# Holding ScalarE's splits of late weights behind squares and results, and moving one Strassen product to the ring of four PSUM banks

## The chip, the core and the metric

The kernel runs on one core of a Trainium2 chip. The metric is the device time of one execution in microseconds (us). Before the change the median of three runs is 2169.33 us (2167.87 to 2173.09).

## What is computed

A decoder trunk of two layers on 512 prompt tokens and 8 × 8 sample tokens (T = 576 columns), model width 1024. The reference, cut to the part around the change:

```python
def decoder_layer(x, pos, states, lw):
    y, new_states = token_mixing(_rmsnorm(x, lw['attn_norm']), pos, states, lw)
    x = x + y.astype(x.dtype)                 # y = merged @ w_out
    h = _rmsnorm(x, lw['ffn_norm'])
    g, u = jnp.split(h @ lw['w_ffn_in'], 2, axis=-1)
    x = x + ((jax.nn.silu(g) * u) @ lw['w_ffn_out']).astype(x.dtype)
    return x, new_states
```

`w_ffn_in` is 1024 × 5632, `w_ffn_out` 2816 × 1024. Token mixing has four recurrent mixers; the change does not touch them.

## The kernel before, in words

Activations lie transposed: 128 channels on the partitions, tokens along the row, in two halves of HW = 288 columns. Every product is made of float16 parts: a weight or activation is split into a high half (ScalarE, L227, L247, L1695) and a low half (VectorE, L228, L249, L1696), and TensorE adds three products, high·high, high·low and low·high (L240 to L242, L1726 to L1728). A full 128 × 128 block of weights therefore costs three matmuls of 288 columns per half.

**Weights.** `wload` (L207) brings a matrix of `nk` blocks in groups of 512 columns of 128 rows: a DMA on SP's queue into one of four `raw` tiles (L219), ScalarE's split (L227) and VectorE's low half (L228), which frees the raw tile. The split tiles come from rings of SBUF ("w" 4, "gs" 6, "r2" 4, "gd" 4, "u" 23, "rd" 2).

**Around the change, per layer, in the order of the program:**

- `out_proj` (L1562): eight row blocks m of `w_out`, two halves each. `part(m, w, half)` makes 24 matmuls into a bank of ring "b" (tile `ob`); `add_x` (L1550) then adds the residual on VectorE (L1553), squares on ScalarE (`sq`, L430), and VectorE adds the squares up (L435). Blocks 0 to 3 go half by half, then blocks 4 to 7 first half, then blocks 4 to 7 second half. The first three FFN matrices (`ffn_weights`, gate and up columns, four groups each) are loaded ahead of the last eight parts.
- `norm_half` (L453): one matmul with ones over the sum of squares (`rps`, L446), a table load pinned to its place in ScalarE's queue (L439), Ln and Exp, a second table load, then eight tiles of `h` (VectorE L469, ScalarE L470, low half on VectorE or GpSimd L471). For the first half it is traced behind part (4, second half).
- `ffn` (L1759): FFN blocks 0 to 2 with plain matmuls (`up`, tile `fb`), 48 per half; after the first the norm of the second half and GpSimd's differences of the activations (`strassen_tokens`). Blocks 3 to 21 are "units" of a Strassen scheme (`strassen`, L1716) with seven products of 12 matmuls, A11, A12, A22, S2, S1, S3, S4, each into one PSUM bank, and seven sums on VectorE (`plus`, L1742, tiles `su` and `sc`). A11 is copied out by ScalarE (L1747), S1's bank is read by u4 and c22, A22's by c21. The unit's weights come from `strassen_weights` two units ahead (load) and in the course of the unit before and the unit itself (seven splits, L1695 and L1696; two accumulating DMAs and two sums on GpSimd). `gated` (L1765) makes silu(g)·u on ScalarE (L1771) and VectorE (L1773) and splits it (L247, L249).
- The down stage: `weights(m)` is a `wload` of one row block of `w_ffn_out` (22 blocks in six groups), `down(m, w, half)` 66 matmuls per half (tile `xb`).

PSUM has eight banks: ring "b" of four, "g" of two, "r" of two. In the FFN's Strassen units A11, A12 and S2 take "b", A22 and S1 "g", S3 and S4 "r". `last_gates` calls the same function for the mixers' gates.

**What sets the order.** The program is traced as above, but the framework's scheduler writes each engine's queue: it runs the trace through a model of the times and takes the instruction that comes first in the program among those that the model has ready. An instruction whose inputs the model sees early moves up in its engine's queue. On the chip every queue is executed in order. `keep_in_program_order` adds an edge of order (not a wait) to the instruction traced before on the same engine; `add_manual_dep` with `NoSync` adds such an edge to a chosen instruction.

Of the kernel before, what the change touches and what calls it, by code (L numbers as in the profile page):

```python
# [25 lines left out]
KT = D // 128  # L26
WS = 256.0
# [121 lines left out]
def result(steps):  # L149

    while True:
        try:
            next(steps)
        except StopIteration as e:
            return e.value
# [18 lines left out]
class Net:  # L174
# [29 lines left out]
        return self.pc[:, c:c + 1]  # L204


    def wload(self, pieces, nk, ncols, rings=("w",)):  # L207


        nc = self.nc  # L210
        step = GW // ncols
        tiles, parts = [], []
        for g, k0 in enumerate(range(0, nk, step)):
            kn = min(step, nk - k0)
            n = kn * ncols
            raw = self.wp.tile([128, GW], F32, tag="raw", name="raw")
            rv = raw[:, :n].rearrange("p (k c) -> p k c", k=kn)
            for ap, off, w in pieces:
                nc.sync.dma_start(out=rv[:, :, off:off + w],  # L219
                                  in_=ap[128 * k0:128 * (k0 + kn)].rearrange("(k p) c -> p k c", p=128))  # L220
            if not parts:
                ring, rings = rings[0], rings[1:] or rings
                c = SIZE[ring] // (4 * GW)
                hl = self.t(ring, [128, c, 2, GW], "whl", F16)
                parts = [hl[:, i] for i in range(c)]
            hl = parts.pop(0)
            nc.scalar.activation(hl[:, 0, :n], raw[:, :n], AF.Copy, scale=WS)  # L227
            nc.vector.scalar_tensor_tensor(hl[:, 1, :n], raw[:, :n], WS, hl[:, 0, :n], op0=MUL, op1=SUB)  # L228
            tiles.append(hl[:, :, :n].rearrange("p a (k c) -> p a k c", k=kn))
        return lambda k: (tiles[k // step][:, 0, k % step], tiles[k // step][:, 1, k % step])  # L230
# [13 lines left out]
    def split(self, out_hi, out_lo, src, scale=1.0):  # L244

        nc = self.nc
        nc.scalar.activation(out_hi, src, AF.Copy, scale=scale)  # L247
        if scale == 1.0:
            nc.vector.tensor_tensor(out_lo, src, out_hi, op=SUB)  # L249
        else:  # L250
            nc.vector.scalar_tensor_tensor(out_lo, src, scale, out_hi, op0=MUL, op1=SUB)
# [1233 lines left out]
    def last_gates(self, l):  # L1485
# [34 lines left out]
        for i, (q, bi, name, m) in enumerate(pairs):  # L1520
            if i + 1 < len(pairs):
                next(prep[i + 1])

            def steps():
                for s in range(7):
                    if s < 4:
                        next(prep[i])
                    if s > 2 and i + 1 < len(pairs):
                        next(prep[i + 1])
                    yield  # L1530
            c = yield from self.strassen(self.sw[i], lambda j, k: [self.T4[2 * j + k // 2][:, k % 2, p] for p in range(2)],
                                         steps(), "b" if q == 2 else "r", "e", lambda a: nc.scalar.activation(a, a, AF.Tanh, scale=0.5 * PH))
            nwb = branch(pairs[i + 1][1], pairs[i + 1][3]) if i + 1 < len(pairs) else None
            for j, half in ((0, 0), (1, 1), (1, 0), (0, 1)):
                hs = slice(half * HW, half * HW + HW)
                th, mg = c[2 * j + half], self.mg[m + j]
                if q == 3 and half == j:
                    self.mh[m + j] = self.t("rs" if m < 6 else "u", [128, 2, T], f"mh{m + j}", F16)
                ps = self.psum("b", [128, HW], "ub")
                run(self.gemm(ps, lambda k: wb[k], range(2), 128 * j, 128, self.hl_rhs(self.bo[name], half)))  # L1540
                u = self.t("e", [128, HW], "gu")
                nc.vector.scalar_tensor_tensor(u, th, 1.0, ps, op0=ADD, op1=MUL)  # L1542
                nc.gpsimd.tensor_tensor(mg[:, hs], mg[:, hs], u, op=ADD)
                if q == 3:
                    mh = self.mh[m + j]
                    self.split(mh[:, 0, hs], mh[:, 1, hs], mg[:, hs], 0.5 * PA * AS)
                yield
            wb = nwb
# [13 lines left out]
    def out_proj(self, l):  # L1562

        nc, t = self.nc, self.io

        def weights(m, rings):
            return self.wload([(t["w_out"][l][:, 128 * m:128 * m + 128], 0, 128)], KT, 128, rings)

        def part(m, w, half):
            ps = self.psum("b", [128, HW], "ob")  # L1570
            run(self.gemm(ps, w, range(KT), 0, 128, self.hl_rhs(self.mh, half)))
            self.add_x(m, half, ps, True)
        for m in range(4):
            self.load_x(m)
            w = weights(m, ("w",))
            for half in range(2):
                part(m, w, half)
        ws = {}
        for m in range(4, KT):
            self.load_x(m)  # L1580
            ws[m] = weights(m, ("gd",))
        self.wf = [self.ffn_weights(l, m, r) for m, r in enumerate(("w", "gs", "r2"))]
        for half in range(2):
            for m in range(4, KT):
                part(m, ws[m], half)
                if half == 1 and m == 4:
                    self.norm_half("ffn_norm_w", l, 0, True)

    def ffn_weights(self, l, m, ring):
        return [self.wload([(self.io["w_ffn_in"][l][:, o + 128 * m:o + 128 * m + 128], 0, 128)], KT, 128, (ring,))  # L1590
                for o in (0, DFF)]

    def mix_units(self, l, then=None):
# [119 lines left out]
            split(name, a)  # L1713
            yield

    def strassen(self, w, t, prep, ps3, ring, then=None):  # L1716


        nc = self.nc
# [17 lines left out]
        def tt(i):  # L1737
            return lambda k: t(i, k)
# [9 lines left out]
        c11 = plus(p1, (yield from product("b", "A12", b(4, h0))), "sc11")  # L1748
        p4 = yield from product("g", "A22", tt(3))
        u2 = plus(p1, (yield from product("b", "S2", tt(1))), "su2", SUB)  # L1750
        p5 = yield from product("g", "S1", tt(0))
        u4 = plus(u2, p5, "su4")
        u3 = plus(u2, (yield from product(ps3, "S3", tt(2))), "su3")
        c22 = plus(u3, p5, "sc22")
# [4 lines left out]
    def ffn(self, l):  # L1759
# [56 lines left out]
        for m in range(3, nm):  # L1816
            if len(prep) > 2:
                next(prep[2])
            now, then = prep[0], prep[1] if len(prep) > 1 else None
            prep.pop(0)  # L1820

            def steps():
                for q in range(7):
                    if q < 4:
                        next(now)
                    if q > 2 and then:
                        next(then)
                    yield
            w = self.sw[m]
            g0, g1, u0, u1 = result(self.strassen(w, lambda i, k: (T4[i][:, k, 0], T4[i][:, k, 1]), steps(), "r", "gt"))  # L1830
            gated(m, 0, g0, u0)
            gated(m, 1, g1, u1)

        def weights(m, rings=("w",)):
            return self.wload([(t["w_ffn_out"][l][:, 128 * m:128 * m + 128], 0, 128)], nm, 128, rings)

        def down(m, w, half, then=None):
            ps = self.psum("b", [128, HW], "xb")
# [112 lines left out]
```

## Time and profile before

| | |
|---|---|
| median of three runs | 2169.33 us |
| the profiled execution, its own time | 2174.78 us |
| its span in the profile | 2173.0 us |
| `out_proj`, layers 0 and 1: first and last matmul of `ob` | 647.0 to 702.1, ending 1769.8 in layer 1 |
| Strassen units of the FFN, to the first matmul of `xb` in layer 0 | 745.4 to 960.2 |

The page of the profile gives busy times per engine; PE is TensorE, DVE VectorE, ACT ScalarE, POOL GpSimd, SP the engine that issues most DMAs. "Idle before" is the time in which an engine waited ahead of an instruction, and the name behind the arrow is what ended that wait. PEclk is the granted share of TensorE's 2.4 GHz, which switches between 1.2 and 2.4.

### The profile page before, as it was taken

To read this page: it belongs to the slowest core of one execution; us is meant where nothing else is said; L and a number is where in the kernel's file an instruction comes from. 1 tells how busy PE (TensorE), PEld (TensorE's weight loads), DVE (VectorE), ACT (ScalarE), POOL (GpSimd) and SP (SyncE) were. 2 spreads that over 40 slices of the span, in tenths; PEclk is the share of its full clock that TensorE was granted. 3 is DMA by queue.
4 is the path that set the end of the run, shared out by engine and by line. 5 is a ranking of instruction groups with operands and counts; after the bars stand their busy time and mean duration, and the time that the engine had idled before them with its cause. 6 is when DMAs were issued, how large, how long until landed. Compare 5 with 4: busy or idle time off the path is not lost.

```text
span 2173.0 us, 42394 instructions
## 1 busy us (share of the span) xinstructions
PE 2028.8 (93%) x15754; PEld 1603.7 (74%) x15754; DVE 1587.5 (73%) x3385; ACT 1089.7 (50%) x2534; POOL 630.3 (29%) x889
## 2 busy tenths in 40 slices
PE   7999999998998999999999899989898989989998
PEld 5777887786777677777777678768776767767776
DVE  7888757668786899863488986675778678998441
ACT  6564546355555555442466455463755455554332
POOL 2213222136541534310012132213464224332000
PEclk9999999999999999999999999999999999999999
DMA  6312214324545455453421222242354544554431
GB/s 183 80 47 63 69 50 112 87 75 107 133 121 174 102 139 134 106 142 111 117 74 51 60 72 57 74 118 62 85 137 116 151 128 112 141 136 108 124 110 49
DMA packets 381274, 223.68 MB, mean 103 GB/s; under 512 B 60674, under 2 KB 361274, under 8 KB 381068
## 3 DMA queue, kind: packets, MB, share of 16 engines
q1 hardware_dynamic: 365516, 192.66, 31.6%
q0 software_dynamic: 15552, 28.32, 7.6%
q8 instruction: 124, 2.03, 0.4%
q14 instruction: 82, 0.67, 0.1%
HBM read 173.65 MB, written 16.59 MB: 88 GB/s over the span
## 4 chain that ended last, share of the span: by engine, by line
PE 50%; DVE 22%; ACT 9%; issue 8%; DMA 6%; POOL 2%; SPq 1%; DVEq 0%; ACTq 0%; POOLq 0%
PE pb L242 5%; PE pb L241 5%; PE pb L240 5%; PE xb L241 4%; PE xb L242 4%; PE xb L240 4%; PE fsS L1728 2%; PE fsS L1726 2%; PE fsS L1727 2%; DVE fy L1773 2%; DVE hA L1696 2%; DVE hS L1696 2%; DVE sc L1742 2%; DVE su L1742 2%; PE lvp L1018 2%
## 5 line engine op out<-in xcount | busy, mean ns | idle before, releaser
L240 PE MATMUL pb<-h,whl 128*128 128x288 f16 (+1 forms) x1504 | 433.7, 289 | 4.0 <-ACT whl L227 2.1
L242 PE MATMUL pb<-h,whl 128*128 128x288 f16 (+1 forms) x1504 | 434.0, 289 | 3.2 <-DVE whl L228 3.1
L241 PE MATMUL pb<-h,whl 128*128 128x288 f16 (+1 forms) x1504 | 433.9, 289 | 0.4 <-DVE h L471 0.2
L228 DVE SCALAR_TENSOR_TENSOR whl<-raw,whl 128x512 f16<-128x512 f32 (+1 forms) x352 | 243.1, 699 | 138.9 <-ACT whl L227 137.0
L242 PEld LDWEIGHTS <-whl 128*128 128x128 f16 (+1 forms) x2784 | 274.2, 98 | 85.4 <-issue 9.2
L241 PEld LDWEIGHTS <-whl 128*128 128x128 f16 (+1 forms) x2784 | 273.7, 98 | 82.0 <-issue 6.0
L240 PEld LDWEIGHTS <-whl 128*128 128x128 f16 (+1 forms) x2784 | 276.2, 99 | 76.4 <-issue 3.6
L227 ACT ACTIVATE whl<-raw 128x512 f16<-128x512 f32 (+1 forms) x352 | 212.7, 617 | 171.7 <-PE pb L242 50.4
L241 PE MATMUL xb<-fa,whl 128*128 128x288 f16 x704 | 201.6, 286 | 0.0
L240 PE MATMUL xb<-fa,whl 128*128 128x288 f16 x704 | 201.6, 286 | 0.0
L242 PE MATMUL xb<-fa,whl 128*128 128x288 f16 x704 | 201.6, 286 | 0.0
L1726 PE MATMUL fsS<-st,hS 128*128 128x288 f16 x456 | 132.5, 291 | 6.9 <-ACT hS L1695 6.9
L1726 PE MATMUL fsA<-h,hA 128*128 128x288 f16 x432 | 123.7, 286 | 12.2 <-DVE gu L1542 10.0
L1728 PE MATMUL fsS<-st,hS 128*128 128x288 f16 x456 | 132.4, 290 | 0.4 <-DVE hS L1696 0.3
L1727 PE MATMUL fsS<-st,hS 128*128 128x288 f16 x456 | 132.5, 291 | 0.0
L1728 PE MATMUL fsA<-h,hA 128*128 128x288 f16 x432 | 123.7, 286 | 0.8 <-DVE hA L1696 0.8
L1727 PE MATMUL fsA<-h,hA 128*128 128x288 f16 x432 | 123.7, 286 | 0.0
L1695 ACT ACTIVATE hS<-sraw 128x512 f16<-128x512 f32 x130 | 79.8, 623 | 63.3 <-POOL sraw L1710 42.5
L1726 PEld LDWEIGHTS <-hS 128*128 128x128 f16 x864 | 85.5, 99 | 34.9 <-ACT hS L1695 12.9
L1696 DVE SCALAR_TENSOR_TENSOR hS<-sraw,hS 128x512 f16<-128x512 f32 x130 | 103.5, 800 | 9.2 <-ACT hS L1695 8.3
L1696 DVE SCALAR_TENSOR_TENSOR hA<-sraw,hA 128x512 f16<-128x512 f32 x110 | 96.6, 888 | 13.1 <-ACT hA L1695 13.1
L1728 PEld LDWEIGHTS <-hS 128*128 128x128 f16 x864 | 85.3, 99 | 24.8 <-DVE hS L1696 2.4
(481 smaller groups left out, 5172.8 us busy)
## 6 DMA issues: line engine op xcount, KB each, us to landing
raw<-in_w_in SPq DMA_DIRECT2D x208, 256.0 KB
sraw<-in_w_ffn_in SPq DMA_DIRECT2D x40, 512.0 KB
raw<-in_w_ffn_out SPq DMA_DIRECT2D x80, 256.0 KB
raw<-in_w_ffn_in SPq DMA_DIRECT2D x78, 256.0 KB
sraw<-sraw POOLq DMA_DIRECT2D x40, 256.0 KB, 3.6
x<-xd SPq DMA_DIRECT2D x32, 288.0 KB
raw<-sraw POOLq DMA_DIRECT2D x34, 256.0 KB, 3.3
sraw<-in_w_in SPq DMA_DIRECT2D x32, 256.0 KB
```

The costliest lines, as they stand in the source:

```text
L227: nc.scalar.activation(hl[:, 0, :n], raw[:, :n], AF.Copy, scale=WS)
L228: nc.vector.scalar_tensor_tensor(hl[:, 1, :n], raw[:, :n], WS, hl[:, 0, :n], op0=MUL, op1=SUB)
L240: nc.tensor.matmul(ps, wh, hi, start=i == 0, stop=False)
L241: nc.tensor.matmul(ps, wh, lo, start=False, stop=False)
L242: nc.tensor.matmul(ps, wl, hi, start=False, stop=i == len(ks) - 1)
L1018: nc.tensor.matmul(ps[:n, hpt * j:hpt * j + hpt, :n // 2], kt[:, j], qt[:, hpt * j:hpt * j + hpt, :n // 2], start=True, stop=True)
L1695: nc.scalar.activation(hl[:, 0], a, AF.Copy, scale=WS)
L1696: nc.vector.scalar_tensor_tensor(hl[:, 1], a, WS, hl[:, 0], op0=MUL, op1=SUB)
L1726: nc.tensor.matmul(ps, w[a][:, 0, k], hi, start=k == 0, stop=False)
L1727: nc.tensor.matmul(ps, w[a][:, 0, k], lo, start=False, stop=False)
L1728: nc.tensor.matmul(ps, w[a][:, 1, k], hi, start=False, stop=k == 3)
L1742: nc.vector.tensor_tensor(o, a, p, op=op)
```

## The change

Three edits. `wload` gets two arguments: `pin` keeps each high split in program order on ScalarE, and `behind` puts an edge of order from each high split but the first group's to a given instruction. In `out_proj` the three FFN matrices are traced at three places among the last eight parts and pinned there, and the first half's norm is traced one part later; in `ffn` the first down matrix's splits, all but the first, are held behind the last split of an FFN result. In `strassen` the ring of S1's product becomes an argument: "b" in the FFN, "g" as before in `last_gates`.

```diff
-    def wload(self, pieces, nk, ncols, rings=("w",)):
+    def wload(self, pieces, nk, ncols, rings=("w",), pin=False, behind=None):
...
-            nc.scalar.activation(hl[:, 0, :n], raw[:, :n], AF.Copy, scale=WS)
+            hi = nc.scalar.activation(hl[:, 0, :n], raw[:, :n], AF.Copy, scale=WS)
+            if g and behind:
+
+                self.tc.add_manual_dep(hi.ins, behind.ins.name, mybir.DependencyInfo(
+                    mybir.DependencyClass.NoSync, mybir.DependencyReason.DATA), reason="order")
+            if pin:
+                self.tc.keep_in_program_order(hi)
...
-        nc.scalar.activation(out_hi, src, AF.Copy, scale=scale)
+        self.last_split = nc.scalar.activation(out_hi, src, AF.Copy, scale=scale)
...
-                                         steps(), "b" if q == 2 else "r", "e", lambda a: nc.scalar.activation(a, a, AF.Tanh, scale=0.5 * PH))
+                                         steps(), "g", "b" if q == 2 else "r", "e", lambda a: nc.scalar.activation(a, a, AF.Tanh, scale=0.5 * PH))
...
-        self.wf = [self.ffn_weights(l, m, r) for m, r in enumerate(("w", "gs", "r2"))]
+        self.wf = []
+        rings = iter(("w", "gs", "r2"))
         for half in range(2):
             for m in range(4, KT):
+                if (half, m) in ((0, 6), (1, 4), (1, 6)):
+                    self.wf.append(self.ffn_weights(l, len(self.wf), next(rings)))
                 part(m, ws[m], half)
-                if half == 1 and m == 4:
+                if half == 1 and m == 5:
                     self.norm_half("ffn_norm_w", l, 0, True)
...
-        return [self.wload([(self.io["w_ffn_in"][l][:, o + 128 * m:o + 128 * m + 128], 0, 128)], KT, 128, (ring,))
+        return [self.wload([(self.io["w_ffn_in"][l][:, o + 128 * m:o + 128 * m + 128], 0, 128)], KT, 128, (ring,), True)
...
-    def strassen(self, w, t, prep, ps3, ring, then=None):
+    def strassen(self, w, t, prep, ps2, ps3, ring, then=None):
...
-        p5 = yield from product("g", "S1", tt(0))
+        p5 = yield from product(ps2, "S1", tt(0))
...
-            g0, g1, u0, u1 = result(self.strassen(w, lambda i, k: (T4[i][:, k, 0], T4[i][:, k, 1]), steps(), "r", "gt"))
+            g0, g1, u0, u1 = result(self.strassen(w, lambda i, k: (T4[i][:, k, 0], T4[i][:, k, 1]), steps(), "b", "r", "gt"))
...
+        last = self.last_split
+
         def weights(m, rings=("w",)):
-            return self.wload([(t["w_ffn_out"][l][:, 128 * m:128 * m + 128], 0, 128)], nm, 128, rings)
+            return self.wload([(t["w_ffn_out"][l][:, 128 * m:128 * m + 128], 0, 128)], nm, 128, rings,
+                              behind=last if m == 0 else None)
```

## Rows read from the trace of the kernel before

**Rows 1.** The page, part 1: busy us, share of the span, instructions.

```profile
PE 2028.8 (93%) x15754; PEld 1603.7 (74%) x15754; DVE 1587.5 (73%) x3385; ACT 1089.7 (50%) x2534; POOL 630.3 (29%) x889
```

**Rows 2.** TensorE's waits, whole span: total us, times, longest us.

```profile
PE fsA L1726 <- DVE sc L1742: 19.0, 19, 1.6
PE rps L446 <- DVE sq L435: 12.6, 3, 6.8
PE fsS L1726 <- ACT hS L1695: 11.7, 4, 3.7
```

**Rows 3.** TensorE's timeline, end of `out_proj`: start, us, instruction, count, idle before.

```profile
691.19 1.33 PE L446 MATMUL rps<-sq,cst 128*128 128x288 f32 x2 [5.57 <-DVE sq L435]
...
701.97 0.29 PE L240 MATMUL fb<-h,whl 128*128 128x288 f16 x1
...
1758.09 1.33 PE L446 MATMUL rps<-sq,cst 128*128 128x288 f32 x2 [6.84 <-DVE sq L435]
...
1769.59 0.29 PE L240 MATMUL fb<-h,whl 128*128 128x288 f16 x1
```

**Rows 4.** ScalarE's timeline, the norm's first table load in layers 0 and 1.

```profile
692.06 1.28 ACT L439 ACT_TABLE_LOAD   x1
...
1758.96 1.28 ACT L439 ACT_TABLE_LOAD   x1
```

**Rows 5.** Groups by line, 658 to 692 us: count, busy, mean ns, idle before.

```profile
L227 ACT ACTIVATE whl<-raw 128x512 f16<-128x512 f32 x22 | 13.3, 625 | 14.4 <-DMA raw<-in_w_ffn_in 7.4 <-DMA raw<-in_w_out 7.0
...
L228 DVE SCALAR_TENSOR_TENSOR whl<-raw,whl 128x512 f16<-128x512 f32 x22 | 15.0, 690 | 10.9 <-ACT whl L227 10.6
```

**Rows 6.** Windows behind four stalls: length, busy per engine, PEclk, DMA share, GB/s.

```profile
692.00:695.00 3.00, 3.00 (x18) 1.86 (x16) 1.09 (x3) 2.92 (x5) 0.00 (x0) 0.66 0.14 51
941.00:947.00 6.00, 5.63 (x25) 3.33 (x26) 5.94 (x11) 4.86 (x11) 1.64 (x1) 0.53 0.48 139
1759.00:1763.00 4.00, 4.00 (x20) 2.50 (x19) 2.17 (x5) 3.93 (x6) 0.00 (x0) 0.58 0.10 37
2006.00:2012.00 6.00, 5.13 (x27) 3.34 (x28) 5.94 (x12) 5.11 (x11) 1.53 (x1) 0.72 0.51 150
```

**Rows 7.** TensorE's timeline, next-to-last Strassen unit of each layer.

```profile
941.31 0.42 PE L1726 MATMUL fsS<-st,hS 128*128 128x288 f16 x1 [3.75 <-ACT hS L1695]
...
2006.56 0.30 PE L1726 MATMUL fsS<-st,hS 128*128 128x288 f16 x1 [3.12 <-ACT hS L1695]
```

**Rows 8.** Timelines of VectorE and ScalarE, last Strassen units of layer 0.

```profile
932.46 2.21 DVE L228 SCALAR_TENSOR_TENSOR whl<-raw,whl 128x512 f16<-128x512 f32 x1
...
938.17 0.63 ACT L227 ACTIVATE whl<-raw 128x512 f16<-128x512 f32 x1 [7.68 <-DMA raw<-in_w_ffn_out]
...
942.83 0.62 ACT L1695 ACTIVATE hS<-raw 128x512 f16<-128x512 f32 x1
...
962.16 0.44 ACT L247 ACTIVATE fa<-fy 128x288 f16<-128x288 f32 x1 [0.53 <-DVE fy L1773]
```

**Rows 9.** Windows of the Strassen stages: length, busy PE, PEld, DVE, ACT, POOL, then PEclk.

```profile
775.00:885.00 110.00, 100.14 (x806) 78.43 (x805) 105.38 (x174) 55.41 (x114) 41.96 (x38) 1.00 0.57 135
885.00:935.00 50.00, 50.00 (x410) 39.84 (x409) 43.43 (x80) 22.29 (x50) 17.84 (x16) 1.00 0.45 107
1853.00:1951.00 98.00, 88.88 (x716) 69.58 (x715) 92.05 (x153) 48.81 (x101) 37.46 (x34) 1.00 0.58 138
```

**Rows 10.** Timelines of VectorE and TensorE, one unit: c22, first matmuls of A22 and S1.

```profile
815.04 0.45 DVE L1742 TENSOR_TENSOR sc<-su,fsS 128x288 f32<-128x288 f32 x1
...
815.54 0.28 PE L1726 MATMUL fsA<-st,hA 128*128 128x288 f16 x1 [1.22 <-DVE sc L1742]
...
818.48 0.29 PE L1726 MATMUL fsS<-st,hS 128*128 128x288 f16 x1
```

**Rows 11.** Timelines of GpSimd and VectorE: last low halves of the first half's `h`.

```profile
701.21 0.73 POOL L471 TENSOR_TENSOR h<-x,h 128x288 f16<-128x288 f32 x1 [1.28 <-ACT h L470]
...
1767.56 0.81 DVE L471 TENSOR_TENSOR h<-x,h 128x288 f16<-128x288 f32 x2
```

## The prediction

> **What bounds the kernel now.** I read the page's busy times first. TensorE is busy 2028.8 us of a 2173.0 us span [rows 1], so whatever the change brings must come out of the 144 us in which TensorE idles, and out of matmuls that run at the lower clock. The list of TensorE's waits says which idle time belongs to the edited lines [rows 2]: the norm's sum `rps` waits 12.6 us for VectorE's sums of squares, A22's product (`fsA`, L1726) waits 19.0 us in 19 units for VectorE's results `sc`, and `fsS` waits 11.7 us for ScalarE's `hS`. These three are what the three parts of the change touch; the other 100 us lie in lines that it leaves alone.
>
> **Where each wait comes from.** TensorE's timeline has `rps` of the first half after 5.57 us of idling in layer 0 and 6.84 us in layer 1 [rows 3]. ScalarE's timeline has the table load that the norm needs, and that stands behind a square, only at 692.06 and 1758.96 [rows 4]. By the groups of this stretch, ScalarE's 22 splits sat idle for 14.4 us on transfers of `w_ffn_in` and `w_out`, and VectorE's low halves for 10.6 us on ScalarE [rows 5]: the queues run in order, so residual adds and squares are queued behind pieces of weights that nobody needs yet. After each such wait the granted clock is lower: 0.66 over 3 us and 0.58 over 4 us, the share of the full 2.4 GHz that a mix with 1.2 GHz gives [rows 6].
>
> The `hS` wait is two stalls, 3.75 us at 941.31 and 3.12 us at 2006.56 [rows 7]. ScalarE stood 7.68 us before the third piece of the first down weights, whose transfer could start only when VectorE had ended the second piece's low half (2.21 us from 932.46); the last FFN result was split later, at 962.16 [rows 8]. The clock afterwards was 0.53 over 6 us and 0.72 over 6 us [rows 6].
>
> The A22 waits lie from 775 to 885 and from 1853 to 1951. VectorE is busy 105.38 of 110 us and 92.05 of 98 there, TensorE 100.14 and 88.88; from 885 to 935 TensorE is at 50.00 of 50 [rows 9]. In one unit A22 starts after 1.22 us, when `c22` (`sc<-su,fsS`, 815.04 plus 0.45) has freed S1's bank; the product S1 follows 2.94 us later [rows 10].
>
> **Part 1, the splits in `out_proj`.** The first matrix's four splits go behind the square of part (5, first half), the second's behind that of (7, first half), the third's behind the norm's last cast; the norm moves one part later. No instruction is added, only places in ScalarE's queue change; SP's loads of the third matrix and of unit 4 wait longer for raw tiles, hidden because unit 4's are first used in the Strassen stage, behind the six passes of `fb`. Removed from TensorE's path: 5.57 us plus 3 us × (1 − 0.66) = 1.0, so 6.6 in layer 0; 6.84 plus 4 × (1 − 0.58) = 1.7, so 8.5 in layer 1 [rows 3, 6]. What is late next is the norm itself. (4, second half) ends at 691.19 − 5.57 = 685.6; the norm now comes after (5, second half), 24 matmuls or 2.94 us later [rows 10], and its table load is pinned behind that part's square, about 1 us on: 689.6, only 2.5 us before 692.06; in layer 1 it is 1755.2, 3.8 us before 1758.96 [rows 4]. The last tile of `h` was ready at 701.21 + 0.73 and 1767.56 + 0.81 [rows 11], so then at 699.5 and 1764.6. `fb` could start at 701.97 − 6.6 = 695.4 and 1769.59 − 8.5 = 1761.1 [rows 3]; its first 24 matmuls would end at 698.3 and 1764.0, but the last three cannot end before 699.9 and 1765.0: waits of 1.6 and 1.0 us. TensorE is so 5.0 and 7.5 us early, the chain of ScalarE and VectorE 2.5 and 3.8. Which one the rest follows the trace cannot say, because the second half's norm starts from TensorE but shares VectorE with everything else. I take the middle: 3.75 + 5.65 = **9.4 us**. Low end: the chain rules and the third matrix's four low halves (0.69 each, 2.8 [rows 5]), done before `rps` until now, come on top: 6.3 − 5.6 = 0.7. High end: everything, 15.1.
>
> **Part 2, the splits behind the last result.** Two stalls go, 6.87 us, and the low clock after them, 6 × 0.47 + 6 × 0.28 = 4.5: 11.4 us; both are followed by stretches in which TensorE sets the pace, so they count in full. The held pieces cost at the new place. Piece 0 is not held: 12 matmuls, 1.47 us, from the end of the last product. Piece 1's split can start when the last result's split (962.16) has left ScalarE, about 962.5, and ends at 963.1; TensorE, at its present 960.2 start, would need it at 961.7, and VectorE's half 0.7 later: about 2.0 us per layer. If the scheduler puts the other half's 12 matmuls into the gap, 0.5. I take 1.2, twice: 11.4 − 2.4 = **9.0 us**. Later pieces come every 0.5 to 0.7 us against 1.47 us of matmuls and cost nothing; that cover is gone if their transfers are late (second rival). Ends: 10.4, and 5.4 if the gap is 3 us with a dip of the clock.
>
> **Part 3, S1's bank.** A22 now shares its two banks with nobody and does not wait for `c22`; S1 waits for it instead if it comes too early. Without the 1.22 us S1 would start at 818.48 − 1.22 = 817.26, 1.77 us after `c22` ended at 815.49 [rows 10]. TensorE can get 1.77 us further ahead of VectorE and then waits again, because VectorE, at 96% and 94% [rows 9], does the same work per unit. 1.77 per layer is kept, since VectorE has slack after 885 in which to catch up: **3.5 us**. High end: all of VectorE's idle time there, 4.6 + 6.0 = 10.6. Low end −2: ring b loses its spare bank, and no row shows what four products on four banks do.
>
> The repeated gap of about 1 us at A22 is also a case for a rule. The Trainium skill, "Perfetto Trace Analysis", section "Identifying Performance Opportunities", says that the same gap repeating on the engine that should be saturated can mean too few buffers in PSUM. By that rule the bank is the bound and part 3 gives its whole 19.0 us; by the rows of VectorE, 3.5. I go by the rows, and keep the other as a rival.
>
> **Sum.** 9.4 + 9.0 + 3.5 = 21.9 us. The profiled execution took 2174.78 us, 1.78 outside its span; 2152.9 would remain of it. It lies 5.45 us above the median of 2169.33, so I take the difference alone: 2147.4, given as 2147. Layer 1's mixing stage is scheduled anew from another state; I put nothing for it.
>
> **Rivals.**
> - VectorE bounds everything from the norm to 885 us. For: its 94 to 96%. Against: it idles 4 to 6% and TensorE leads in places. Then part 1 gives 0.7, part 3 nothing, part 2 its 9.0: 2159.6. Chance 0.24.
> - Slower: the held pieces arrive one at a time at the head of the down stage. A piece took 3.5 us from the freed tile (934.67) to its split, 0.63 for that and 0.69 for the low half [rows 8]: 4.8 us against 1.47. Five pieces cost 16.7 us per layer, 33.3 in all, against gains of 9.4 + 11.4 + 3.5 = 24.3: 2178. It decides from four late pieces per layer on. Against it: unit 20 releases three raw tiles with its splits up to 942.83 [rows 8], some 19 us before they are needed. Chance 0.06.
> - The pins free no square, because pieces of `w_out`, which are not pinned, hold them just as well (7.0 of the 14.4 us [rows 5]). Part 1 gives nothing: 2156.8. Chance 0.12.
> - The bank is the bound: 15.5 us more, 2131.9. VectorE's rows speak against it. Chance 0.06.
>
> **Numbers.** The forecast keeps 0.52. Its own terms reach from 2133 (all high ends) to 2165 (all low ends); a range from 2136 to 2165 takes in the first and third rival and cuts off the slower one and most of the fourth. A measurement of this kernel can tell about 0.3%, 6.5 us: faster ends at 2162.8. The forecast, the fourth and most of the first and third lie below: 0.83. Within 0.3%: low ends of the first and third rival, 0.11. Slower: the second, 0.06.
>
> **What would show it.** Right: `rps` without idle time and no dip of the clock after it; no wait of ScalarE for `w_ffn_out` before the last FFN result; five splits in a row after it with a gap of 0.5 to 2 us at the first `xb`; A22 without waits, S1 with a shorter sum of them. Wrong: waits of `rps` on squares as long as before; S1 waiting as long as A22 did with VectorE unchanged (then part 3 is nothing); ScalarE waiting for DMA among the five; a mixing stage of layer 1 that differs by more than 5 us.

## The result and the profile after

The changed kernel takes 2148.68 us (median of 4 runs, 2145.01 to 2149.68), the kernel before, beside it, 2168.60 us (4 runs). The ratio of the two is 0.9889, 95% interval 0.9872 to 0.9906: faster by 1.1%, 24.1 us by the ratio and 19.9 by the medians. Forecast was a gain of 21.9 us, to 2147. The profiled execution took 2149.09 us, its span is 2147.1.

First the page's busy times, and from the list of TensorE's waits (total us, times, longest us) the rows that answer to [rows 1, 2]. Below the edits every line number has grown: L446 is now L453, L1726 L1736, L1742 L1752, L227 L228, L240 to L242 L247 to L249.

```profile
PE 2022.0 (94%) x15754; PEld 1603.7 (75%) x15754; DVE 1587.1 (74%) x3385; ACT 1087.3 (51%) x2533; POOL 633.1 (29%) x889
```

```profile
PE fsS L1736 <- DVE sc L1752: 9.5, 14, 0.8
PE fsS L1736 <- ACT hS L1705: 4.8, 2, 2.5
PE fb L248 <- POOL h L478: 4.3, 5, 2.0
PE fb L248 <- DVE h L478: 4.2, 6, 1.8
...
PE rps L453 <- DVE sq L442: 0.8, 2, 0.6
...
PE xb L247 <- ACT whl L228: 0.5, 2, 0.3
PE fsA L1736 <- DVE sc L1752: 0.2, 1, 0.2
```

The norm's 12.6 us are 0.8. The 11.7 us of `hS` are 4.8, and those two waits lie in `last_gates`; none is left in the FFN. A22's 19.0 us are 0.2, but S1 has 9.5 in their place. VectorE does the same 3385 instructions in the same time. TensorE's busy time falls by 6.8 us at the same 15754 matmuls; that fits the low clock that is gone, 7.2 us by the windows of the prediction. The windows behind the former stalls show it (columns as in [rows 6]; the first and third stand behind `rps`, the second before the first `xb`), and the last two answer to [rows 9]:

```profile
692.00:695.00 3.00, 3.00 (x27) 2.38 (x26) 1.17 (x4) 2.94 (x4) 0.00 (x0) 1.00 0.37 115
941.00:947.00 6.00, 6.00 (x51) 4.79 (x49) 4.41 (x10) 1.87 (x5) 0.00 (x0) 1.00 0.20 77
1743.00:1747.00 4.00, 4.00 (x35) 3.21 (x33) 1.60 (x5) 3.77 (x5) 0.00 (x0) 1.00 0.38 118
...
775.00:885.00 110.00, 104.40 (x841) 82.05 (x840) 106.01 (x176) 56.35 (x117) 42.73 (x39) 1.00 0.58 138
...
1853.00:1951.00 98.00, 92.69 (x744) 72.55 (x743) 92.72 (x161) 49.05 (x104) 35.30 (x32) 1.00 0.53 124
```

The granted clock is 1.00 where it was 0.66, 0.53 and 0.58; in the fourth window, 0.72 before, it is 1.00 too (1992 to 1998). From 775 to 885 TensorE is busy 104.40 us instead of 100.14, VectorE 106.01 instead of 105.38: still 96%.

TensorE's timeline at the norm (as [rows 3]): `rps` starts without idle time, and `fb` follows.

```profile
690.59 0.65 PE L453 MATMUL rps<-sq,cst 128*128 128x288 f32 x2
...
696.96 0.29 PE L247 MATMUL fb<-h,whl 128*128 128x288 f16 x1
...
1742.02 0.65 PE L453 MATMUL rps<-sq,cst 128*128 128x288 f32 x2
...
1748.38 0.29 PE L247 MATMUL fb<-h,whl 128*128 128x288 f16 x1
```

`rps` is also shorter, 0.65 us against 1.33, and the first table load is at 691.80 in layer 0.

The stage marks, first matmuls read from TensorE's timelines of both profiled executions, say where the time went:

| stage | layer 0 before, after | layer 1 before, after | gained |
|---|---|---|---|
| first `ob` to first `fb` | 55.00, 47.80 | 57.29, 47.81 | 7.2 + 9.5 |
| first `fb` to A22 of the first unit | 47.50, 50.54 | 46.72, 50.41 | −3.0 − 3.7 |
| that A22 to first `xb` | 210.72, 199.77 | 208.59, 199.65 | 10.9 + 8.9 |
| first `xb` to the end of the last | 130.01, 130.55 | 137.14, 137.69 | −0.5 − 0.5 |

Together 28.8 us. The mixing stages, which the change leaves alone, took 2.2 us more ahead of layer 0 and 0.7 more ahead of layer 1; that makes the 25.9 us between the spans.

At the head of the down stage, ScalarE's and then TensorE's timeline in layer 0 (start, us, instruction, count, idle before):

```profile
949.24 0.44 ACT L254 ACTIVATE fa<-fy 128x288 f16<-128x288 f32 x1 [0.53 <-DVE fy L1783]
949.59 2.17 ACT L228 ACTIVATE whl<-raw 128x512 f16<-128x512 f32 x4
953.19 0.42 ACT L228 ACTIVATE whl<-raw 128x256 f16<-128x256 f32 x1 [1.43 <-DMA raw<-in_w_ffn_out]
```

```profile
950.26 0.30 PE L247 MATMUL xb<-fa,whl 128*128 128x288 f16 x1 [0.25 <-ACT whl L228]
```

Four held splits stand behind the last result's split without a pause; the fifth, of half the size, waits 1.43 us for its transfer, and nobody waits for it. TensorE loses 0.25 us.

### The profile page after: what moved, and what is told of

Same layout as the page of the kernel before. It is cut to its first block, busy times and chain, and to the rows that moved or that the text cites. A ratio compares the mean times of both kernels' runs of the same rounds, so it can differ in the third digit from the quotient of the medians.

```text
span 2147.1 us, 42408 instructions
## 1 busy us (share of the span) xinstructions
PE 2022.0 (94%) x15754; PEld 1603.7 (75%) x15754; DVE 1587.1 (74%) x3385; ACT 1087.3 (51%) x2533; POOL 633.1 (29%) x889
## 4 chain that ended last, share of the span: by engine, by line
PE 58%; DVE 20%; ACT 8%; issue 6%; DMA 4%; POOL 2%; SPq 1%; DVEq 0%; ACTq 0%; POOLq 0%
PE pb L249 5%; PE pb L247 5%; PE pb L248 5%; PE xb L249 4%; PE xb L247 4%; PE xb L248 4%; PE fsS L1736 3%; PE fsS L1738 3%; PE fsS L1737 3%; PE fsA L1736 2%; PE fsA L1737 2%; PE fsA L1738 2%; PE lvp L1025 2%; DVE hS L1706 1%; DVE su L1752 1%
## 5 line engine op out<-in xcount | busy, mean ns | idle before, releaser
L247 PE MATMUL pb<-h,whl 128*128 128x288 f16 (+1 forms) x1504 | 434.0, 289 | 3.3 <-ACT whl L228 1.4
L249 PE MATMUL pb<-h,whl 128*128 128x288 f16 (+1 forms) x1504 | 434.1, 289 | 2.4 <-DVE whl L235 2.4
L249 PEld LDWEIGHTS <-whl 128*128 128x128 f16 (+1 forms) x2784 | 274.3, 99 | 86.9 <-issue 12.6
L235 DVE SCALAR_TENSOR_TENSOR whl<-raw,whl 128x512 f16<-128x512 f32 (+2 forms) x352 | 239.1, 692 | 128.3 <-ACT whl L228 126.3
L247 PEld LDWEIGHTS <-whl 128*128 128x128 f16 (+1 forms) x2784 | 276.4, 99 | 75.3 <-issue 3.6
L228 ACT ACTIVATE whl<-raw 128x512 f16<-128x512 f32 (+2 forms) x352 | 210.8, 615 | 150.2 <-PE pb L249 49.0
L247 PE MATMUL xb<-fa,whl 128*128 128x288 f16 x704 | 201.3, 286 | 0.5 <-ACT whl L228 0.5
L249 PE MATMUL xb<-fa,whl 128*128 128x288 f16 x704 | 201.2, 286 | 0.0
L1736 PE MATMUL fsS<-st,hS 128*128 128x288 f16 x456 | 130.3, 286 | 10.7 <-DVE sc L1752 9.5
L1736 PE MATMUL fsA<-h,hA 128*128 128x288 f16 x432 | 124.2, 288 | 15.5 <-DVE gu L1549 11.2
L1738 PE MATMUL fsS<-st,hS 128*128 128x288 f16 x456 | 130.4, 286 | 0.0
L1737 PE MATMUL fsS<-st,hS 128*128 128x288 f16 x456 | 130.4, 286 | 0.0
L1736 PEld LDWEIGHTS <-hS 128*128 128x128 f16 x864 | 84.8, 98 | 26.5 <-ACT hS L1705 5.5
```

Source lines behind the costliest of these rows:

```text
L228: hi = nc.scalar.activation(hl[:, 0, :n], raw[:, :n], AF.Copy, scale=WS)
L247: nc.tensor.matmul(ps, wh, hi, start=i == 0, stop=False)
L249: nc.tensor.matmul(ps, wl, hi, start=False, stop=i == len(ks) - 1)
L1736: nc.tensor.matmul(ps, w[a][:, 0, k], hi, start=k == 0, stop=False)
L1737: nc.tensor.matmul(ps, w[a][:, 0, k], lo, start=False, stop=False)
L1738: nc.tensor.matmul(ps, w[a][:, 1, k], hi, start=False, stop=k == 3)
```

## The experiments

Times are ratios to the kernel before on the same chip (its median there was 2172 to 2175 us); a difference in us is the ratio's difference times that median. Where two changed kernels are set beside each other, both ratios have an interval, so such a difference is known to some 5 us.

### One part alone

**The bank.**

```diff
-        p5 = yield from product("g", "S1", tt(0))
+        p5 = yield from product(ps2, "S1", tt(0))
```

with `ps2` "b" in the FFN and "g" elsewhere.

> The kernel before with the bank of S1 alone. VectorE sets the pace of the units (my step): A22's 19.0 us of waits go, S1 waits for c22 in its place for some 10 to 12 us in all, VectorE's share in the stretch stays above 94%, and the kernel is 3.5 us shorter (2 to 6); the traces of before and after, less the 11.4 us of part 2, leave 8.5 us for it. The bank is the bound (rival): neither A22 nor S1 waits more than 3 us in all, and the kernel is 16 to 19 us shorter.

Measured: 0.9969 (0.9954 to 0.9983), 6.7 us faster, by the interval 3.7 to 10.0. The profiled execution, 2156.24 us, is the fastest of the twelve (median 2167.15), so only its waits and distances are used, not its time. TensorE's waits:

```profile
PE fsS L1726 <- DVE sc L1742: 9.3, 14, 0.8
...
PE fsA L1726 <- DVE sc L1742: 0.2, 1, 0.2
```

The waits for VectorE's `sc` fall from 19.0 us to 9.5 and lie ahead of S1: more than the 3.5 us of the prediction, far less than 19.0.

**The splits behind the last result.**

```diff
+            if g and behind:
+                self.tc.add_manual_dep(hi.ins, behind.ins.name, mybir.DependencyInfo(
...
+                               behind=last if m == 0 else None)
```

> The kernel before with the first down matrix's splits held behind the last FFN result, alone. My step: both hS stalls (3.75 and 3.12 us) and the low clock behind them go, 11.4 us, and the first xb product loses 0.5 to 2 us per layer: 9 us shorter (8 to 11). If the stall is only passed on to A22 or S1, because VectorE was late anyway: under 4 us. If the held pieces come late: no shorter, with waits of ScalarE on the DMA of w_ffn_out of over 5 us per layer at the start of xb.

Measured: 0.9958 (0.9942 to 0.9974), 9.1 us faster. A22's waits are untouched, the `hS` waits of the FFN are gone, and 0.5 us stands ahead of `xb`, as in the changed kernel:

```profile
PE fsA L1729 <- DVE sc L1745: 19.0, 19, 1.6
...
PE fsS L1729 <- ACT hS L1698: 4.9, 2, 2.5
```

**The pins and the later norm.**

```diff
+                if (half, m) in ((0, 6), (1, 4), (1, 6)):
+                    self.wf.append(self.ffn_weights(l, len(self.wf), next(rings)))
                 part(m, ws[m], half)
-                if half == 1 and m == 4:
+                if half == 1 and m == 5:
```

> The kernel before with the pinned places of the three FFN matrices and the norm one part later, alone. My step: rps without idle time in both layers, TensorE at the first fb 7 to 9 us earlier counted from the first ob, of which 3 to 4 us are lost again up to the first A22 of the units, 9.4 us shorter in all (8 to 11). VectorE bounds everything up to the end of the units (rival): the start of the units comes earlier, but the A22 waits grow by as much, and the kernel is 0 to 3 us shorter.

Measured: 0.9963 (0.9949 to 0.9976), 8.0 us faster. `rps` waits 0.8 us, A22 as before:

```profile
PE fsA L1731 <- DVE sc L1747: 18.3, 20, 1.4
...
PE rps L448 <- DVE sq L437: 0.8, 2, 0.6
```

The stage from `ob` to `fb` takes 47.8 us in both layers, that from `fb` to A22 50.5 and 50.8: 16.7 us gained, 7.1 given back at once. The three parts make 0.31 + 0.42 + 0.37 = 1.10%; the whole change makes 1.11%. The four intervals together leave some 0.3%, or 6.6 us: within that, the parts neither help nor hinder one another.

### Inside part 1

**The norm's place.**

```diff
-                if half == 1 and m == 5:
+                if half == 1 and m == 4:
```

> The changed kernel with the first half's norm traced behind part (4, second half) again; the matrices stay at their new places and pinned. My theory (part 1 was sized by a chain that starts at the table load): TensorE's norm sum now stands one part (2.94 us) earlier and the four low halves of the second matrix no longer lie ahead of its squares' sum, so the sum finds them ready but for at most 2 us per layer; the table load comes about 2 us earlier and the waits inside the first 48 matmuls of fb shrink by as much: 0 to 3 us faster than the changed kernel, 2146 to 2149 beside its 2149. Rival 1 (the later place is what removed the wait): the sum waits 4 us or more per layer again with a low clock after it, and 5 to 10 us of the gain are lost, 2154 to 2159. Rival 2 (the place is indifferent): within 1 us, waits of the sum under 1 us.

Measured: 0.9892 (0.9875 to 0.9909), by the time the same as the whole change, 0.7 us apart and known to some 5. My expectation that the waits inside `fb` shrink was wrong. `ob` to `fb` takes 47.8 us again, since `fb` cannot start before the last `ob`; but the second half's `rps` waits (3.3 us in all, 3 times), and `fb` waits longer for its second half:

```profile
PE fb L248 <- DVE h L478: 7.8, 10, 2.7
...
PE rps L453 <- DVE sq L442: 3.3, 3, 1.7
```

First `fb` to A22 takes 53.8 and 53.0 us, 5.8 more in the two layers than in the changed kernel. The ratio doesn't show them, and they lie at the edge of what it can tell; so by the marks the later place helps, and by the time it is open.

**The pin.**

```diff
-        return [self.wload([(self.io["w_ffn_in"][l][:, o + 128 * m:o + 128 * m + 128], 0, 128)], KT, 128, (ring,), True)
+        return [self.wload([(self.io["w_ffn_in"][l][:, o + 128 * m:o + 128 * m + 128], 0, 128)], KT, 128, (ring,))
```

> The changed kernel with the three FFN matrices traced at their new places but not pinned. My theory (the pin holds the pieces behind the squares, the place alone doesn't): the scheduler floats the pieces ahead of the squares again, the norm's sum waits 3 us or more per layer and the clock falls behind it; 4 to 9 us of part 1's 8.0 are lost, 2153 to 2158. Rival 1 (tracing the matrices later is enough, since the scheduler cannot take an instruction before its tiles are free and its transfer is issued): waits of the sum under 1 us, 2148 to 2150. Rival 2: the later place without a pin is worse than the kernel before in this stretch, over 10 us lost.

Measured: 0.9916 (0.9899 to 0.9934), 5.9 us slower than the whole change. In layer 1 the wait is back, half as long as in [rows 3]; in layer 0 it is 1.73 us:

```profile
1752.70 1.33 PE L453 MATMUL rps<-sq,cst 128*128 128x288 f32 x2 [3.36 <-DVE sq L442]
```

From first `ob` to A22 of the first unit it takes 103.0 and 103.4 us, where the changed kernel takes 98.3 and 98.2 and the kernel before 102.5 and 104.0. So by these marks part 1 needs the pin, and the later place alone gives next to nothing. The time agrees, but the two intervals overlap, and the 5.9 us are known to some 5 only.

### Inside part 2

**The first piece held as well.**

```diff
-            if g and behind:
+            if behind:
```

> The changed kernel with the first piece of the first down matrix held behind the last FFN result as well (six pieces instead of five). What is asked: what the held pieces cost at their new place, and why it was 0.5 us a layer and not 1.2. My theory: the 12 matmuls of the first piece, together with the other half's, cover the five splits that come one after another behind the last result's split (949.24 in layer 0); without that cover the first matmul of xb, now at 947.27, waits for the first piece until about 950.2: 2.5 to 3.5 us per layer with a low clock behind it, 5 to 9 us slower than the changed kernel, 2154 to 2158 beside its 2149. Rival (the scheduler fills the place with something else, or TensorE's later pieces were the limit anyway): under 2 us slower, with a wait at the first xb under 1 us per layer.

Measured: 0.9923 (0.9906 to 0.9941), 7.4 us slower than the whole change. The first `xb` of layer 0, where TensorE waits 2.83 us, as it does in layer 1:

```profile
952.49 0.42 PE L247 MATMUL xb<-fa,whl 128*128 128x288 f16 x1 [2.83 <-ACT whl L228]
```

The free first piece is what hides the others. In the changed kernel TensorE does 21 matmuls, by its records, from 947.27 on before it waits 0.25 us for the second; here it has none to do. The granted clock was 0.54 in the 3 us behind the wait of layer 0; behind that of layer 1, equally long, it was 1.00 (2007.4 to 2010.0).

### What paces the Strassen units

**VectorE relieved, in the kernel before and in the changed one.** Both leave out the low halves of the FFN results, and `xb` takes the high half in their place:

```diff
-            self.split(act[m][:, 0, hs], act[m][:, 1, hs], y)
+            nc.scalar.activation(act[m][:, 0, hs], y, AF.Copy)
...
-            for i, _ in enumerate(self.gemm(ps, w, range(nm), 0, 128, self.hl_rhs(act, half))):
+            for i, _ in enumerate(self.gemm(ps, w, range(nm), 0, 128, lambda k: (act[k][:, 0, half * HW:half * HW + HW],) * 2)):
```

> The kernel before without the low halves of the FFN results (L249): VectorE has two instructions of 0.45 us less in each unit, the down products take the high half in the place of the low one, TensorE's work is the same. VectorE sets the pace (my theory): without any change of banks the A22 waits fall from 19.0 us to under 5, and the kernel is 14 to 20 us shorter. The bank is the bound (rival): c22 frees it at nearly the same distance behind its product, the A22 waits stay above 14 us, and the kernel is under 5 us shorter.

> The changed kernel without the low halves of the FFN results (two of 0.45 us per unit leave VectorE); the down product takes the high half twice, so TensorE's work is the same and the results lack their low halves. Theory A (VectorE's work per unit, 94% busy with what GpSimd's sums add to it, is what S1 still waits for): S1's 9.5 us of waits fall under 2 us, and the time falls by 8 to 12 us, to 2137 to 2141. Theory B (four products on four banks bound TensorE now): S1's waits stay above 6 us and the time falls by less than 4 us.

Measured: 0.9915 (0.9897 to 0.9932) on the kernel before, 18.5 us faster with its banks as they were, and 0.9826 (0.9807 to 0.9845) on the changed one, 13.7 us faster still than the whole change, rather more than expected. First the kernel before, then the changed one:

```profile
PE fsS L1726 <- ACT hS L1695: 6.6, 8, 2.5
PE fsA L1726 <- DVE sc L1742: 6.0, 12, 1.0
```

```profile
PE fsS L1736 <- DVE sc L1752: 1.1, 4, 0.3
```

```profile
775.00:885.00 110.00, 109.05 (x888) 86.69 (x887) 100.53 (x163) 56.13 (x120) 44.14 (x40) 1.00 0.59 140
```

On the kernel before, A22's waits fall from 19.0 us to 6.0, but they aren't the whole of the 18.5 us: both `hS` stalls of [rows 7] are gone as well. Of the 6.6 us 4.9 lie in `last_gates`, and the longest wait left in the FFN is 0.55. Part 2 alone, which removes these stalls, was worth 9.1 us. Why they went here was not tested, so the price of VectorE's work is read from the changed kernel, which has no such stalls: 13.7 us.

There, with 0.9 us less of VectorE's work per unit, TensorE is busy 109.05 of 110 us (third fence, the window of the changed kernel). So four products on four banks don't hold TensorE back: VectorE does.

**S3 beside A22, in the changed kernel.**

```diff
-        u3 = plus(u2, (yield from product(ps3, "S3", tt(2))), "su3")
+        u3 = plus(u2, (yield from product("g" if ps2 == "b" else ps3, "S3", tt(2))), "su3")
```

> The changed kernel with S3's product in the ring of two that A22 uses, which leaves the other ring of two to S4 alone; in the FFN only. What is asked: why part 3 gave 6.7 us and not 3.5, and whether more banks would give more. Theory A (VectorE's work per unit sets the pace, the banks only set how far TensorE runs ahead): a spare bank elsewhere changes the lead by a product or less; S1's waits stay between 7 and 12 us in all and the time within 2 us of the changed kernel, 2147 to 2151. Theory B (banks are still the bound): S1 waits on sums that also free other banks, so a change of rings moves the waits by half or more, either to under 5 us (2140 to 2144) or to another product with 5 us more (2154 and above).

Measured: 0.9897 (0.9881 to 0.9914), 1.7 us slower than the whole change, as theory A has it; but the waits are neither theory's. A22 waits again, 17.5 us in all and now for `u3`; the waits, and below them TensorE's and VectorE's timeline:

```profile
PE fsA L1736 <- DVE su L1752: 17.5, 18, 1.7
```

```profile
844.68 0.28 PE L1736 MATMUL fsA<-st,hA 128*128 128x288 f16 x1 [0.97 <-DVE su L1752]
...
844.18 0.44 DVE L1752 TENSOR_TENSOR su<-su,fsS 128x288 f32<-128x288 f32 x1
...
844.66 0.45 DVE L1752 TENSOR_TENSOR sc<-su,fsS 128x288 f32<-128x288 f32 x1
```

A22 starts at 844.68, when `u3` has ended (844.18 + 0.44) and `c22` (844.66 to 845.11) hasn't. This is what showed me my error in part 3. A recurring wait on VectorE is paid in every unit wherever it stands; a bank decides only **how far into its unit TensorE stands when it waits**. By that rule this run should be slower than the changed kernel, by 24 matmuls less the 0.49 us from the end of `u3` to that of `c22`: 2.45 us per layer, 4.9 in all. The ratio gives 1.7, known to some 5, and so decides nothing on it.

**The mirror image, in the kernel before.**

```diff
-        p4 = yield from product("g", "A22", tt(3))
+        p4 = yield from product(psa, "A22", tt(3))
```

with `psa` "b" in the FFN and "g" elsewhere.

> The kernel before with the mirror image of part 3 alone: A22's product takes a bank of the ring of four and S1 keeps the ring of two to itself; the same number of banks per product as in the run with part 3 alone. My theory, corrected after the runs so far: a wait on VectorE recurs in every unit wherever it stands, and what a bank is worth is how much further in the unit TensorE may stand when it waits, measured from the end of c22. With S1 in the ring of four that was 24 matmuls, 2.94 us per layer, 5.9 in all (6.7 measured). Here a ring hands out the bank that came free first, so A22 takes S2's and S2 takes the one that c21 frees 0.37 us after c22, 12 matmuls or 1.47 us behind A22: a lead of 1.1 us per layer, 2.2 us in all, ratio about 0.999, with waits of 14 us or more in which the name of a sum stands ahead of S2. Rival (each of the two products with a ring of its own is what counts, whichever of them moves): 6 to 7 us faster than before, ratio about 0.997, waits of 10 to 11 us as in the run with part 3 alone.

Measured: 0.9988 (0.9977 to 0.9999), 2.6 us faster; 2.2 was expected by the lead, 6 to 7 by the count of banks, which lies outside the interval. S2 waits for `c21` (812.13 + 0.45), 12 matmuls behind A22:

```profile
PE fsS L1726 <- DVE sc L1742: 13.9, 16, 1.2
```

```profile
812.63 0.28 PE L1726 MATMUL fsS<-st,hS 128*128 128x288 f16 x1 [1.16 <-DVE sc L1742]
...
812.13 0.45 DVE L1742 TENSOR_TENSOR sc<-su,fsA 128x288 f32<-128x288 f32 x1
```

### Two attempts at a faster kernel

Both start from the changed kernel and take work off VectorE's path.

```diff
-            self.split(act[m][:, 0, hs], act[m][:, 1, hs], y)
+            self.last_split = nc.scalar.activation(act[m][:, 0, hs], y, AF.Copy)
+            nc.gpsimd.tensor_tensor(act[m][:, 1, hs], y, act[m][:, 0, hs], op=SUB)
```

> The changed kernel with the low halves of all FFN results (0.45 us each on VectorE, two per unit, 44 per layer) on GpSimd. My theory (VectorE's work per unit is the bound, about 94% busy, and GpSimd, some 38% busy there, has room): 0.9 us per unit leave VectorE, S1's 9.5 us of waits fall under 4 us, the time falls by 4 to 9 us, 2140 to 2145. Rival 1 (GpSimd becomes late): its queue runs in order and carries the sums and the accumulating transfers of the splits S2 to S4; results then hold these up, TensorE waits for hS, and the time is 2 us or more above the changed kernel, over 2151. Rival 2 (the two engines slow one another): VectorE's operations get longer by as much as is taken away, and the time stays within 2 us, 2147 to 2151.

Measured: 0.9964 (0.9951 to 0.9976), some 16 us slower than the changed kernel. TensorE's waits for VectorE's results grow from 9.7 to 22.8 us, and VectorE is as busy as ever with 25 instructions fewer (waits, window, and VectorE's groups by line of this run from 775 to 885):

```profile
PE fsS L1736 <- DVE sc L1752: 15.0, 16, 1.3
...
PE fsA L1736 <- DVE sc L1752: 7.8, 8, 1.2
```

```profile
775.00:885.00 110.00, 100.01 (x803) 78.26 (x802) 104.45 (x151) 53.31 (x111) 57.17 (x54) 1.00 0.55 132
```

```profile
L1706 DVE SCALAR_TENSOR_TENSOR hA<-sraw,hA 128x512 f16<-128x512 f32 x17 | 26.9, 1580 | 1.4 <-ACT hA L1705 1.4
L1706 DVE SCALAR_TENSOR_TENSOR hS<-raw,hS 128x512 f16<-128x512 f32 x15 | 22.1, 1470 | 0.7
```

In the changed kernel these two groups take 774 and 1103 ns each; `fy` alone got shorter, 451 ns for 1017. TensorE waits for `hS` in `last_gates` only, 4.8 us as in the changed kernel, so rival 1 fell. Rival 2 is right, and too mild.

```diff
-        nc.gpsimd.tensor_tensor(a22, a22, a11, op=ADD)
+        add(a22, a11)
```

> The changed kernel with one of GpSimd's two sums per unit (a22 plus a11, 1.4 to 1.6 us) made by an accumulating transfer, like the two sums that are so made already. What is asked: whether the stretch of VectorE's splits, 2.3 us beside a GpSimd sum where 0.68 us stands without one, is what puts VectorE behind. Theory A (the two engines exclude one another while both read SBUF): about half of the 28 us per layer by which VectorE's splits and products are longer than their shortest form goes, S1's waits fall from 9.5 to under 5 us, and the time falls by 3 to 8 us, 2141 to 2146; it would be a kernel faster than both. Rival 1 (the transfer is late: S3's split waits for it, and TensorE for hS): 2 us or more slower, over 2151. Rival 2 (issuing a transfer from GpSimd holds VectorE as long as the sum does): within 2 us, VectorE's mean durations unchanged.

Measured: 1.0334 (1.0312 to 1.0355), some 97 us slower than the changed kernel. ScalarE's and VectorE's groups, 775 to 945 and 775 to 885, columns as in [rows 5], then the transfer's issues (count, KB, median us to landing):

```profile
L1705 ACT ACTIVATE hS<-sraw 128x512 f16<-128x512 f32 x30 | 17.6, 619 | 45.4 <-DMA sraw<-raw 28.7 <-DMA sraw<-sraw 16.7
...
L1706 DVE SCALAR_TENSOR_TENSOR hS<-sraw,hS 128x512 f16<-128x512 f32 x20 | 13.8, 689 | 27.8 <-ACT hS L1705 27.8
```

```profile
sraw<-raw POOLq DMA_DIRECT2D x50, 256.0 KB, 4.2
```

Theory A's half is there: the split takes 689 ns instead of 883. But the transfer lands 4.2 us after its issue where the sum took some 1.5, and both engines' queues stand behind it. For the splits the mechanism is borne out (`fy` stays long, 1133 ns, beside the sum that is left), and the kernel is useless. Neither attempt beats the changed kernel.

## Why the prediction was right, and where it was not

**Part 1: 9.4 us forecast, 8.0 measured alone (5.2 to 11.1).** Its steps hold. The 6.6 and 8.5 us to be removed were 7.2 and 9.5 in the profiled executions. "What is late next is the norm itself" was right too: `fb` to A22 grew by 3.0 and 3.7 us, so 4.2 and 5.8 us are kept, between the chain's 2.5 and 3.8 and TensorE's 5.0 and 7.5. That they lie near the middle, 3.75 and 5.65, is luck: the middle was a choice between two chains and no step of the sum. `fb`'s waits on VectorE and GpSimd for `h` have risen from 6.3 (4.0 and 2.3) to 8.5 us. The larger share of what was given back the prediction didn't name: `fb` waits 3.0 us for banks that the FFN's results (`fsg`, `fy`) free, where it waited for none, and A11 of the first unit 2.2 us for `fsg` instead of 0.4. The table load came only 0.3 us earlier by the clock of the trace (691.80 for 692.06), but `ob` itself started 2.2 us later; from there it is the 2.5 us of the forecast. The third rival (pieces of `w_out` hold the squares just as well) fell: `rps` waits 0.8 us.

**Part 2: 9.0 us forecast, 9.1 measured alone (5.7 to 12.6).** The stalls and the low clock behind them went as computed. The gap of 1.2 us at `xb` is 0.25, and the down stage grew by 0.5 per layer: 21 matmuls, not 12, stand ahead of it, so matmuls of the other half were put into the gap, which the prediction had as its cheap case. The slower rival fell. Its late piece exists, 1.43 us for the fifth, but one late piece behind four early ones costs nothing.

**Part 3: 3.5 us forecast, 6.7 measured alone (3.7 to 10.0).** This is the term that failed. "TensorE can get 1.77 us further ahead of VectorE and then waits again" takes the distance from A22 to S1, 2.94 us, less the wait of 1.22. But the wait that A22 is spared is part of what is won, and it comes back in a later unit, ahead of S1; what the bank adds is the whole distance between the two, 24 matmuls or 2.94 us per layer, 5.9 in all. The run with A22 moved, where the same rule gives 1.1 us per layer and 2.6 in all was measured, bears this out; by time alone 3.5 lies only just outside the interval.

The traces show it more closely. TensorE's lead is here the distance from the first matmul of S4, behind all these waits, to the end of the same unit's `c21`, read from the timelines of TensorE and VectorE, as the mean of the sixth to twelfth unit in layers 0 and 1:

| kernel | lead | above the kernel before | by the rule | VectorE's time per unit |
|---|---|---|---|---|
| before | 5.94, 5.94 | | | 11.5, 11.5 |
| the bank alone | 8.68, 8.68 | 2.7, 2.7 | 2.94 | 11.4, 11.3 |
| the whole change | 8.69, 8.63 | 2.8, 2.7 | 2.94 | 11.3, 11.3 |
| the whole change with S3 beside A22 | 6.38, 6.22 | 0.4, 0.3 | 0.49 | 11.5, 11.3 |
| the mirror image | 6.85, 6.94 | 0.9, 1.0 | 1.1 | 11.3, 11.4 |

The lead grows by what the rule gives, less at most 0.25 us, and not by 1.77. VectorE's time per unit falls by 2% at most; whether the bank does that or it varies anyway the runs don't show, and what was measured above 5.9 lies within the interval.

In the changed kernel the first wait of layer 0 comes at 812.93 instead of 781.07, three units later.

Behind the sentence on VectorE's rows stood the rule of the Trainium skill ("Perfetto Trace Analysis", "Identifying Performance Opportunities") that a gap repeating on the engine that should be saturated can mean too few buffers. It would have made 19.0 us of part 3. The trace does not agree: a third of that came, and taking 0.9 us per unit from VectorE gave 13.7 us more with the banks as they were. The rule says "can"; here the occupancy of the engine that empties the banks decided.

The sum, 21.9, lies between the 19.9 us of the medians and the 24.1 of the ratio. Part of that is luck as well: part 1's 1.4 us too many make up for some of the 3.2 too few of part 3. The first rival (VectorE bounds everything, part 1 gives 0.7, part 3 nothing) fell at both terms, though its premise, VectorE at 96%, stands to the end: a bound engine is no reason that a lead is worth nothing, as long as it can catch up later, which it does behind 885.

## What to carry to other kernels

When the engine that empties the banks sets the pace, price a bank by the distance between the instruction that waits now and the one that will wait then, once per stretch, and not by the waits that vanish. In this kernel, work that the scheduler moved up because its inputs looked ready was best held behind whatever the critical path needs from the same queue, except for the first piece, whose use hides the rest. Moving work from VectorE to GpSimd is not to be counted as relief until the durations of the other instructions have been looked at.

## What the runs showed of the hardware

VectorE's split of 128 × 512 takes 0.68 us, and mostly 1.5 to 2.5 us where a sum of GpSimd runs beside it. In the Strassen units of the changed kernel all 197 splits without a sum beside them take 0.68 or 0.69 us; of the 43 with one, 32 take 1.52 to 2.48. The same holds for `fy` (L1783): 0.45 us without a sum, 1.52 to 2.15 with one (775 to 885 and 1830 to 1950). VectorE's, GpSimd's and TensorE's timelines of the changed kernel, one unit:

```profile
838.18 0.69 DVE L1706 SCALAR_TENSOR_TENSOR hA<-sraw,hA 128x512 f16<-128x512 f32 x1
...
839.52 2.36 DVE L1706 SCALAR_TENSOR_TENSOR hA<-sraw,hA 128x512 f16<-128x512 f32 x1
842.02 2.34 DVE L1706 SCALAR_TENSOR_TENSOR hS<-sraw,hS 128x512 f16<-128x512 f32 x1
844.28 0.44 DVE L1752 TENSOR_TENSOR su<-sp,fsS 128x288 f32<-128x288 f32 x1
...
846.69 0.45 DVE L1752 TENSOR_TENSOR sc<-su,fsS 128x288 f32<-128x288 f32 x1
```

```profile
839.75 1.57 POOL L1714 TENSOR_TENSOR sraw<-sraw 128x512 f32<-128x512 f32 x1
...
842.23 1.57 POOL L1720 TENSOR_TENSOR sraw<-sraw 128x512 f32<-128x512 f32 x1
```

```profile
844.77 0.28 PE L1736 MATMUL fsS<-st,hS 128*128 128x288 f16 x1 [0.59 <-DVE su L1752]
...
847.20 0.28 PE L1736 MATMUL fsS<-st,hS 128*128 128x288 f16 x1 [0.79 <-DVE sc L1752]
```

Two splits, 2.36 and 2.34 us long, each span a sum of 1.57; VectorE's sums come late, and S2 waits for `u2` and S1 for `c22`. 0.68 + 1.57 = 2.25: the split behaves as if it stood still for the length of the sum. The Trainium skill, "SBUF — State Buffer", "SBUF: two separate sides", says that VectorE and GpSimd share one pair of ports, that an instruction of VectorE with two inputs in SBUF and one of GpSimd that reads SBUF exclude each other, that the one that starts first has the pair for its whole length, and that the other blocks. These rows agree that the split stands still. On who goes first they don't: by the records both splits start 0.2 us ahead of the sum, and they are the ones that grow. What I had not expected is its weight: part of the "busy" time by which VectorE paces this stage is this standing still. From 775 to 885 it is an estimated 24 of 106 us, from the groups' means (883, 1103 and 774 ns for 58 splits, 1017 for 20 `fy`) above 0.68 and 0.45 us each. With one of the two sums gone the split fell to 0.69 us, with more work on GpSimd two of its groups rose to 1.5. A way to make the sums without GpSimd and without a late transfer was not tried.
